# Block inverse of a gated delta net with its four series alternating, and the output transposes moved into the projection (two-layer hybrid attention, one core)

## The chip, the cores and the metric

One core of a Trainium2 chip (trn2) runs the whole program. The metric is the device time of one execution in microseconds (us), given as the median of several executions; the profile comes from one further execution of its own. TensorE is PE in the profile, with its weight loads as PEld, VectorE is DVE, ScalarE is ACT, GpSimd is POOL, and SyncE is SP, which here only issues transfers.

## What is computed

Two layers on x (256 tokens, width 2048), all in fp32. Layer 0 joins a gated delta net (8 heads, run in both directions), a differential attention (8 heads) and a memory attention, and adds their projection to x; layer 1 is sliding-window, latent and memory attention in the same frame. The part that matters here is the delta net of layer 0:

```python
m = jnp.where(strict, jnp.einsum('bhncd,bhnsd->bhncs', k_beta, k) * decay, 0.0)
t_inv = lax.linalg.triangular_solve(eye + m, jnp.broadcast_to(eye, m.shape), left_side=True, lower=True,
                                    unit_diagonal=True)
u = t_inv @ (v * beta[..., None])
w = t_inv @ (k_beta * jnp.exp(g)[..., None])
...
o = rms_norm(o, out_gain) * jax.nn.silu(gate.reshape(bsz, seq, GDN_HEADS, GDN_DV).astype(F32))
...
return x + y @ w_out
```

The kernel takes chunks of 128 tokens, so it inverts a unit triangular 128x128 matrix for each head, direction and chunk. y joins the outputs of the delta net (1024 columns), the differential attention (1024) and the memory attention (512).

## The kernel before

Every weight matrix passes through `load_split`: SP loads 512 KB into `w` (L194, 4 buffers), ACT casts it to `wh` (L201), and DVE forms the rest `wl` (L202; 3 buffers of each). Three matmuls per product, high by high, low by high and high by low, then give fp32 accuracy. `gemm` (L218 to L220), `gate_T` (L361 to L363) and `gemm_out` (L250 to L252) have this form. A scheduler orders the instructions of each engine when the program is built, so that matmuls of these products fill the delta net's waits wherever it sees them free.

The delta net works on 4 heads at a time (`grp` 0, then 1). The inverses of the 32x32 diagonal blocks are computed on DVE in one buffer, `Rm`, and leave for DRAM as `t_d` and `r_d` (L794 to L797). POOL then clears `Rm` (L800), and for each group four transfers bring the blocks back into `Tm` and four into `Rm` (L812): `Tm` holds the transposed inverse, `Rm` the inverse. Two steps build the 128x128 inverse. The first joins pairs of 32x32 blocks: PX (L849, `M8` and `T8` into `px`), a copy to `X1` on DVE (L851), PY (L855, into `py`) with a copy into `T8` on ACT (L857), and PR (L860, into `pr`) with a copy into `R8` on DVE (L862). `M8`, `T8` and `R8` are views of `MnT`, `Tm` and `Rm`. The second step does the same with 64x64 blocks: PA (L869), a copy to `X2` (L870), PB (L875) and a copy into `R8` (L876).

A series is the 8 matmuls of one direction d and one pair of blocks: 4 series in each product of the first step, 2 in each of the second. An fp32 matmul leaves two records in the trace, so a series has 16 and a product of the first step 64. The operands of the four series come from four different groups of 32 partitions. `px` and `py` of one direction share a PSUM bank, and `pr` has another, so that two of the four series always write to one bank.

After the inverse a chain of small products runs in `bank4`: L889 on PE, L898 and L899, L902 (the copy to `St`, ACT), L906, L910, L914, then L919 and L921. L178 (ACT) sums squares, L145 (POOL) takes the root, and L929 writes `o_gdn`, which L348 multiplies by the gate. `gated_T` transposes it (L388) and splits it into `y[0]` and `y[4]` (L154 ACT, L155 DVE). `gemm_out` walks over four groups of 512 columns, and in each over the blocks 8, 12, 16, 0 and 4 of y, in chunks of two k-tiles of 12 matmuls each; blocks 0 and 4 are the delta net's, the others those of the two attentions.

Of the kernel before, what the change touches and what calls it, by code (L numbers as in the profile page):

```python
# [36 lines left out]
R_GDN, R_SUB, R_EMQ, R_EMK, R_OMQ, R_OMK, R_SWQ, R_SWK, R_MLQ, R_MLK, R_DFQ, R_DFK, R_CNV = range(68, 81)  # L37
# [50 lines left out]
def kernel(ctx: ExitStack, tc: tile.TileContext, a: dict, out: bass.AP):  # L88
    nc = tc.nc
    V, A, G, T = nc.vector, nc.scalar, nc.gpsimd, nc.tensor  # L90
# [17 lines left out]
    def ps_tile():  # L108
        return psp.tile([P, 512], F32, tag="ps", name="ps")
# [87 lines left out]
    def load_split(src, kn, n):  # L197
        w = first_w.pop(0) if first_w else load_w(src, kn, n)
        wh = wpool.tile([P, KC * 512], F32R, tag="wh", name="wh")
        wl = wpool.tile([P, KC * 512], F32R, tag="wl", name="wl")  # L200
        A.copy(wh[:, :kn * n], w[:, :kn * n])  # L201
        V.tensor_tensor(wl[:, :kn * n], w[:, :kn * n], wh[:, :kn * n].bitcast(F32), op=ALU.subtract)  # L202
        return (wh[:, :kn * n].rearrange("p (k n) -> p k n", k=kn),
                wl[:, :kn * n].rearrange("p (k n) -> p k n", k=kn))
# [30 lines left out]
                T.matmul(o, lhsT=wl[:, k], rhs=H[:, kk], start=False, stop=kk == NK - 1)  # L235
        return acc

    def gemm_out(wd, y, blocks, evac):

        wv = wd.rearrange("(k p) c -> p k c", p=P)  # L240
        chunks = [(k0, k) for k0 in blocks for k in range(0, 4, KC)]
        for g in range(D // 512):
            acc = [accp.tile([P, 512], F32, tag="acc", name="acc") for _ in range(2)]
            for b, (k0, ks) in enumerate(chunks):
                wh, wl = load_split(wv[:, k0 + ks:k0 + ks + KC, g * 512:(g + 1) * 512], KC, 512)
                for t in range(2):
                    for k in range(KC):
                        h, l = (x_[:, ks + k, t * P:(t + 1) * P] for x_ in y[k0])
                        first, last = b == 0 and k == 0, b == len(chunks) - 1 and k == KC - 1
                        T.matmul(acc[t], lhsT=h, rhs=wh[:, k], start=first, stop=False)  # L250
                        T.matmul(acc[t], lhsT=h, rhs=wl[:, k], start=False, stop=False)  # L251
                        T.matmul(acc[t], lhsT=l, rhs=wh[:, k], start=False, stop=last)  # L252
            for t in range(2):
                evac(g, t, acc[t])
# [127 lines left out]
    def gated_T(o_get, gain, y):  # L382

        for t in range(2):
            pt = accp.tile([P, 512], F32, tag="acc", name="acc")
            o_ = o_get(t)
            for c in range(4):
                T.transpose(pt[:, c * P:(c + 1) * P], o_[:, c * P:(c + 1) * P], ident)  # L388
            src = pt.rearrange("p (c q) -> p c q", c=4)
            split(src, gain, *(x_[:, :, t * P:(t + 1) * P] for x_ in y))  # L390


    par = keep(R_END)
# [283 lines left out]
    o_gdn = opool2.tile([P, 2, 1024], F32, name="o_gdn")  # L677
# [124 lines left out]
    for grp in range(2):  # L802
# [27 lines left out]
        for t in range(2):  # L830
# [3 lines left out]
            for h in range(4):  # L834
# [8 lines left out]
        px, py, pr = [[p_[d].rearrange("p (m c) -> p m c", m=8) for d in range(2)]  # L843
                      for p_ in ([b_[0][:, :S] for b_ in banks], [b_[0][:, S:] for b_ in banks],
                                 [b_[1][:, :S] for b_ in banks])]
        for d in range(2):
            for r_, c_ in rcs[d]:
                for m in range(8):
                    T.matmul(px[d][blk[r_], m], lhsT=M8[d][blk[c_], m, blk[r_]], rhs=T8[d][blk[c_], m, blk[c_]],  # L849
                             start=True, stop=True)  # L850
                V.tensor_copy(X1[d][blk[r_], :, 0:32], px[d][blk[r_]])  # L851
        for d in range(2):
            for r_, c_ in rcs[d]:
                for m in range(8):
                    T.matmul(py[d][blk[r_], m], lhsT=R8[d][blk[r_], m, blk[r_]], rhs=X1[d][blk[r_], m, 0:32],  # L855
                             start=True, stop=True)
                A.copy(T8[d][blk[r_], :, blk[c_]], py[d][blk[r_]])  # L857
            for r_, c_ in rcs[d]:
                for m in range(8):
                    T.matmul(pr[d][blk[c_], m], lhsT=X1[d][blk[r_], m, 0:32], rhs=R8[d][blk[r_], m, blk[r_]],  # L860
                             start=True, stop=True)
                V.tensor_copy(R8[d][blk[c_], :, blk[r_]], pr[d][blk[c_]])  # L862
        rc2 = [(slice(64, 128), slice(0, 64)), (slice(0, 64), slice(64, 128))]
        X2 = [gp.tile([P, 8, 64], F32, tag="X", name="X2", bufs=2) for d in range(2)]
        for d in range(2):
            r_, c_ = rc2[d]
            pa = ps_tile().rearrange("p (m c) -> p m c", m=8)
            for m in range(8):
                T.matmul(pa[r_, m], lhsT=M8[d][c_, m, r_], rhs=T8[d][c_, m, c_], start=True, stop=True)  # L869
            V.tensor_copy(X2[d][r_], pa[r_])  # L870
        for d in range(2):
            r_, c_ = rc2[d]
            pb = ps_tile().rearrange("p (m c) -> p m c", m=8)
            for m in range(8):
                T.matmul(pb[c_, m], lhsT=X2[d][r_, m], rhs=R8[d][r_, m, r_], start=True, stop=True)  # L875
            A.copy(R8[d][c_, :, r_], pb[c_])  # L876

# [55 lines left out]
    def cols512(x_, g):  # L935
        return lambda t: x_[:, t, 512 * g:512 * (g + 1)]
# [16 lines left out]
    with tc.tile_pool(name="yp", bufs=2, reuse_waits="tile") as yp:  # L953
        y = {k: halves(yp, [P, 4, S], f"y{k}", bufs=1) for k in range(0, 20, 4)}
        for g in range(2):
            gated_T(cols512(o_dif, g), par[:, R_SUB:R_SUB + 1], y[8 + 4 * g])
        split(o_mem, None, *y[16])
        for i in range(2):
            gated_T(cols512(o_gdn, i), par[:, R_GDN:R_GDN + 1], y[4 * i])

        ssx = yp.tile([P, 2, 4], F32, name="ssx1", bufs=1)
        nxt = []

        def evac(g, t, ps):
            if not nxt:
                nxt.extend(xpool.tile([P, NK, S], F32R, tag=n, name=n + "1") for n in ("xH", "xL"))
            x_ = x1[:, t, 512 * g:512 * (g + 1)]
            xr = yp.tile([P, 512], F32, tag="xr", name="xr")
            with tc.issue_after(acts[-1].ins):
                A.dma_start(xr, a["xN"][t * P:(t + 1) * P, 512 * g:512 * (g + 1)])  # L970
            V.tensor_tensor(x_, ps, xr, op=ALU.add)
            sum_sq(x_, ssx[:, t, g:g + 1], [P, 512])
            if t == 1:
                split_T(lambda k, t: x1[:, t, k * P:(k + 1) * P], par[:, R_ODN:R_ODN + NK], range(4 * g, 4 * g + 4), *nxt)
        gemm_out(a["ev_w_out"][0], y, (8, 12, 16, 0, 4), evac)
        opool_stack.close()
        xH, xL = nxt
        ss1 = spool.tile([P, 2], F32, tag="ssx", name="ss1")
        V.tensor_reduce(ss1, ssx, axis=AX.X, op=ALU.add)
        inv_sqrt(rs1, ss1, 1.0 / D, EPS)  # L980
# [9 lines left out]
    y = {}  # L990
# [210 lines left out]
```

## Time and profile before

| | us |
|---|---|
| median of 3 runs | 1225.27 (1223.86 to 1230.07) |
| profiled execution | 1225.94 |
| its span in the trace | 1224.2 |
| PE busy | 1203.8 |
| DVE busy | 841.3 |
| ACT busy | 640.8 |
| POOL busy | 107.8 |

The span runs from the first to the last instruction of the trace; the execution's own time lies 1.74 us above it. The mean granted clock of TensorE is 0.992 of full speed. A row of a timeline has start, duration, engine, line, operation, output and inputs, tile and count; rows of one line that follow each other are joined, and brackets name idle time ahead of the row and what ended it.

### The profile page before, as it was taken

How to read it: one execution, taken by the hardware profiler on the slowest of the kernel's cores; microseconds unless marked ns; L12 is line 12 of the kernel's file. 1: busy time of each engine (PE TensorE's matmuls, PEld its weight loads, DVE VectorE, ACT ScalarE, POOL GpSimd, SP SyncE). 2: the span in 40 equal slices, each digit the busy share in tenths (PEclk: the TensorE clock that was granted, in tenths of full speed). 3: DMA queues.
4: the chain of work that ended last, by engine and by line, in shares of the span. 5: the costliest groups of instructions: out<-in, count | busy, mean ns of one | idle time of the engine just before them, and what ended most of it. 6: DMA issues, size and time to landing. Idle time of an engine off the chain costs nothing.

```text
span 1224.2 us, 19860 instructions
## 1 busy us (share of the span) xinstructions
PE 1203.8 (98%) x7608; PEld 1075.8 (88%) x7608; DVE 841.3 (69%) x1450; ACT 640.8 (52%) x1117; POOL 107.8 (9%) x116
## 2 busy tenths in 40 slices
PE   9899999999999999999979999999999999999998
PEld 7678878788999998899968889999889889998887
DVE  6766876576989899738645555577666677776553
ACT  6754755455555454334644445666555455554332
POOL 0110102010001010002000000332200000000000
PEclk9999999999999999989989999999999999999999
DMA  9976766546655676723516656666656565554663
GB/s 339 356 225 227 231 203 180 172 146 181 170 158 137 158 193 189 204 81 91 167 50 208 206 184 165 189 182 191 174 155 207 151 206 160 158 161 165 205 207 120
DMA packets 183184, 221.95 MB, mean 181 GB/s; under 512 B 20537, under 2 KB 119609, under 8 KB 182577
## 3 DMA queue, kind: packets, MB, share of 16 engines
q1 hardware_dynamic: 172640, 201.09, 55.0%
q10 hardware_dynamic: 9552, 16.48, 3.8%
q0 software_dynamic: 896, 3.11, 0.8%
q8 instruction: 59, 0.97, 0.3%
q14 instruction: 37, 0.30, 0.1%
HBM read 214.36 MB, written 6.29 MB: 180 GB/s over the span
## 4 chain that ended last, share of the span: by engine, by line
PE 87%; DMA 5%; DVE 4%; ACT 2%; issue 1%; POOL 0%; SPq 0%; ACTq 0%; DVEq 0%
PE acc L219 13%; PE acc L218 12%; PE acc L220 12%; PE acc L251 6%; PE acc L250 6%; PE acc L252 6%; PE acc L362 4%; PE acc L363 4%; PE acc L361 4%; PE acc L235 3%; PE acc L233 3%; PE acc L234 3%; PE ps L165 3%; DMA w<-in_ev_w_in_dram 2%; PE ps L889 2%; DVE wl L202 2%
## 5 line engine op out<-in xcount | busy, mean ns | idle before, releaser
L202 DVE TENSOR_TENSOR wl<-w,wh 128x1024 fp32r<-128x1024 f32 (+3 forms) x392 | 456.8, 1167 | 246.1 <-ACT wh L201 239.5
L201 ACT CAST wh<-w 128x1024 fp32r<-128x1024 f32 (+3 forms) x392 | 391.9, 1001 | 405.8 <-PE acc L220 138.5
L219 PE MATMUL acc<-wl,xH 128*128 128x512 f32 (+3 forms) x704 | 258.1, 368 | 3.2 <-DVE wl L202 3.2
L220 PE MATMUL acc<-wh,xL 128*128 128x512 f32 (+3 forms) x704 | 254.9, 363 | 0.0
L218 PE MATMUL acc<-wh,xH 128*128 128x512 f32 (+3 forms) x704 | 238.0, 366 | 3.3 <-ACT wh L201 3.3
L219 PEld LDWEIGHTS acc<-wl,xH 128*128 128x128 f32 x704 | 132.3, 188 | 24.0 <-DVE wl L202 5.5
L218 PEld LDWEIGHTS acc<-wh,xH 128*128 128x128 f32 x704 | 129.9, 188 | 21.9 <-ACT wh L201 5.0
L220 PEld LDWEIGHTS acc<-wh,xL 128*128 128x128 f32 x704 | 132.3, 188 | 16.8
L251 PE MATMUL acc<-wl,y 128*128 128x512 f32 x320 | 125.0, 391 | 0.0
L252 PE MATMUL acc<-wh,y 128*128 128x512 f32 x320 | 124.6, 391 | 0.0
L250 PE MATMUL acc<-wh,y 128*128 128x512 f32 x320 | 114.8, 392 | 0.0
L362 PE MATMUL acc<-xL,wh 128*128 128x256 f32 x384 | 110.5, 288 | 0.0
L361 PE MATMUL acc<-xH,wh 128*128 128x256 f32 x384 | 110.4, 288 | 0.0
L235 PE MATMUL acc<-xH,wl 128*128 128x256 f32 x384 | 109.4, 286 | 0.8 <-DVE wl L202 0.8
L363 PE MATMUL acc<-xH,wl 128*128 128x256 f32 x384 | 110.0, 287 | 0.0
L233 PE MATMUL acc<-xH,wh 128*128 128x256 f32 x384 | 109.3, 285 | 0.0
L234 PE MATMUL acc<-xL,wh 128*128 128x256 f32 x384 | 109.1, 284 | 0.0
L145 POOL TENSOR_TENSOR r<-isq,kept 128x4 f32<-128x4 f32 (+2 forms) x27 | 51.2, 1895 | 394.8 <-DVE isq L144 390.2
L362 PEld LDWEIGHTS acc<-xL,wh 128*128 128x128 f32 x384 | 74.7, 194 | 0.4
L361 PEld LDWEIGHTS acc<-xH,wh 128*128 128x128 f32 x384 | 74.7, 195 | 0.2
L235 PEld LDWEIGHTS acc<-xH,wl 128*128 128x128 f32 x384 | 73.4, 191 | 1.4 <-DVE wl L202 1.4
L363 PEld LDWEIGHTS acc<-xH,wl 128*128 128x128 f32 x384 | 74.6, 195 | 0.0
(364 smaller groups left out, 1788.5 us busy)
## 6 DMA issues: line engine op xcount, KB each, us to landing
w<-in_ev_w_in_dram SPq DMA_DIRECT2D x136, 512.0 KB, 4.0
w<-in_od_w_in_dram SPq DMA_DIRECT2D x72, 512.0 KB, 3.7
w<-in_ev_w_out_dram SPq DMA_DIRECT2D x40, 512.0 KB, 3.7
w<-in_od_w_out_dram SPq DMA_DIRECT2D x40, 512.0 KB, 3.7
w<-in_od_w_in_dram SPq DMA_DIRECT2D x32, 384.0 KB, 3.3
w<-in_od_mem_w_kv_dram SPq DMA_DIRECT2D x16, 512.0 KB, 3.6
w<-in_ev_mem_w_kv_dram SPq DMA_DIRECT2D x16, 512.0 KB, 3.7
w<-in_od_w_in_dram SPq DMA_DIRECT2D x16, 288.0 KB, 2.9
```

The lines of the kernel that those rows point to most:

```text
L201: A.copy(wh[:, :kn * n], w[:, :kn * n])
L202: V.tensor_tensor(wl[:, :kn * n], w[:, :kn * n], wh[:, :kn * n].bitcast(F32), op=ALU.subtract)
L218: T.matmul(o, lhsT=h, rhs=wh[:, k], start=first, stop=False)
L219: T.matmul(o, lhsT=h, rhs=wl[:, k], start=False, stop=False)
L220: T.matmul(o, lhsT=l, rhs=wh[:, k], start=False, stop=last)
L235: T.matmul(o, lhsT=wl[:, k], rhs=H[:, kk], start=False, stop=kk == NK - 1)
L250: T.matmul(acc[t], lhsT=h, rhs=wh[:, k], start=first, stop=False)
L251: T.matmul(acc[t], lhsT=h, rhs=wl[:, k], start=False, stop=False)
L252: T.matmul(acc[t], lhsT=l, rhs=wh[:, k], start=False, stop=last)
L361: T.matmul(acc[i], lhsT=wh[:, k, cs], rhs=H[:, kk], start=kk == 0, stop=False)
L362: T.matmul(acc[i], lhsT=wh[:, k, cs], rhs=L[:, kk], start=False, stop=False)
L363: T.matmul(acc[i], lhsT=wl[:, k, cs], rhs=H[:, kk], start=False, stop=kk == NK - 1)
```

## The change

In the block inverse the loops over the heads m and over the series are exchanged, so that the four series of PX, PY and PR, and the two of PA and PB, alternate matmul by matmul. The copies follow when all of a product's series are through. In the projection, `gated_T` of the delta net's output is no longer called ahead of `gemm_out`: `gemm_out` calls it when the first group of columns comes to block 0 and to block 4. The operations, their sizes and their operands stay as they were.

```diff
@@ -235,13 +235,17 @@
                 T.matmul(o, lhsT=wl[:, k], rhs=H[:, kk], start=False, stop=kk == NK - 1)
         return acc
 
-    def gemm_out(wd, y, blocks, evac):
-
+    def gemm_out(wd, y, blocks, evac, late=()):
+
+
+        late = dict(late)
         wv = wd.rearrange("(k p) c -> p k c", p=P)
         chunks = [(k0, k) for k0 in blocks for k in range(0, 4, KC)]
         for g in range(D // 512):
             acc = [accp.tile([P, 512], F32, tag="acc", name="acc") for _ in range(2)]
             for b, (k0, ks) in enumerate(chunks):
+                if k0 in late:
+                    late.pop(k0)()
                 wh, wl = load_split(wv[:, k0 + ks:k0 + ks + KC, g * 512:(g + 1) * 512], KC, 512)
                 for t in range(2):
                     for k in range(KC):
@@ -843,37 +847,36 @@
         px, py, pr = [[p_[d].rearrange("p (m c) -> p m c", m=8) for d in range(2)]
                       for p_ in ([b_[0][:, :S] for b_ in banks], [b_[0][:, S:] for b_ in banks],
                                  [b_[1][:, :S] for b_ in banks])]
-        for d in range(2):
-            for r_, c_ in rcs[d]:
-                for m in range(8):
-                    T.matmul(px[d][blk[r_], m], lhsT=M8[d][blk[c_], m, blk[r_]], rhs=T8[d][blk[c_], m, blk[c_]],
-                             start=True, stop=True)
-                V.tensor_copy(X1[d][blk[r_], :, 0:32], px[d][blk[r_]])
-        for d in range(2):
-            for r_, c_ in rcs[d]:
-                for m in range(8):
-                    T.matmul(py[d][blk[r_], m], lhsT=R8[d][blk[r_], m, blk[r_]], rhs=X1[d][blk[r_], m, 0:32],
-                             start=True, stop=True)
-                A.copy(T8[d][blk[r_], :, blk[c_]], py[d][blk[r_]])
-            for r_, c_ in rcs[d]:
-                for m in range(8):
-                    T.matmul(pr[d][blk[c_], m], lhsT=X1[d][blk[r_], m, 0:32], rhs=R8[d][blk[r_], m, blk[r_]],
-                             start=True, stop=True)
-                V.tensor_copy(R8[d][blk[c_], :, blk[r_]], pr[d][blk[c_]])
-        rc2 = [(slice(64, 128), slice(0, 64)), (slice(0, 64), slice(64, 128))]
+        four = [(d, blk[r_], blk[c_]) for i in range(2) for d in range(2) for r_, c_ in [rcs[d][i]]]
+        for m in range(8):
+            for d, r_, c_ in four:
+                T.matmul(px[d][r_, m], lhsT=M8[d][c_, m, r_], rhs=T8[d][c_, m, c_], start=True, stop=True)
+        for d, r_, c_ in four:
+            V.tensor_copy(X1[d][r_, :, 0:32], px[d][r_])
+        for m in range(8):
+            for d, r_, c_ in four:
+                T.matmul(py[d][r_, m], lhsT=R8[d][r_, m, r_], rhs=X1[d][r_, m, 0:32], start=True, stop=True)
+        for d, r_, c_ in four:
+            A.copy(T8[d][r_, :, c_], py[d][r_])
+        for m in range(8):
+            for d, r_, c_ in four:
+                T.matmul(pr[d][c_, m], lhsT=X1[d][r_, m, 0:32], rhs=R8[d][r_, m, r_], start=True, stop=True)
+        for d, r_, c_ in four:
+            V.tensor_copy(R8[d][c_, :, r_], pr[d][c_])
+        two = [(d, slice(64, 128), slice(0, 64)) if d == 0 else (d, slice(0, 64), slice(64, 128)) for d in range(2)]
         X2 = [gp.tile([P, 8, 64], F32, tag="X", name="X2", bufs=2) for d in range(2)]
-        for d in range(2):
-            r_, c_ = rc2[d]
-            pa = ps_tile().rearrange("p (m c) -> p m c", m=8)
-            for m in range(8):
-                T.matmul(pa[r_, m], lhsT=M8[d][c_, m, r_], rhs=T8[d][c_, m, c_], start=True, stop=True)
-            V.tensor_copy(X2[d][r_], pa[r_])
-        for d in range(2):
-            r_, c_ = rc2[d]
-            pb = ps_tile().rearrange("p (m c) -> p m c", m=8)
-            for m in range(8):
-                T.matmul(pb[c_, m], lhsT=X2[d][r_, m], rhs=R8[d][r_, m, r_], start=True, stop=True)
-            A.copy(R8[d][c_, :, r_], pb[c_])
+        pa, pb = [[ps_tile().rearrange("p (m c) -> p m c", m=8) for d in range(2)] for _ in range(2)]
+        for m in range(8):
+            for d, r_, c_ in two:
+                T.matmul(pa[d][r_, m], lhsT=M8[d][c_, m, r_], rhs=T8[d][c_, m, c_], start=True, stop=True)
+        for d, r_, c_ in two:
+            V.tensor_copy(X2[d][r_], pa[d][r_])
+        for m in range(8):
+            for d, r_, c_ in two:
+                T.matmul(pb[d][c_, m], lhsT=X2[d][r_, m], rhs=R8[d][r_, m, r_], start=True, stop=True)
+        for d, r_, c_ in two:
+            A.copy(R8[d][c_, :, r_], pb[d][c_])
@@ -955,9 +958,6 @@
         for g in range(2):
             gated_T(cols512(o_dif, g), par[:, R_SUB:R_SUB + 1], y[8 + 4 * g])
         split(o_mem, None, *y[16])
-        for i in range(2):
-            gated_T(cols512(o_gdn, i), par[:, R_GDN:R_GDN + 1], y[4 * i])
-
         ssx = yp.tile([P, 2, 4], F32, name="ssx1", bufs=1)
         nxt = []
@@ -972,7 +972,8 @@
             sum_sq(x_, ssx[:, t, g:g + 1], [P, 512])
             if t == 1:
                 split_T(lambda k, t: x1[:, t, k * P:(k + 1) * P], par[:, R_ODN:R_ODN + NK], range(4 * g, 4 * g + 4), *nxt)
-        gemm_out(a["ev_w_out"][0], y, (8, 12, 16, 0, 4), evac)
+        gemm_out(a["ev_w_out"][0], y, (8, 12, 16, 0, 4), evac,
+                 [(4 * i, lambda i=i: gated_T(cols512(o_gdn, i), par[:, R_GDN:R_GDN + 1], y[4 * i])) for i in range(2)])
         opool_stack.close()
         xH, xL = nxt
         ss1 = spool.tile([P, 2], F32, tag="ssx", name="ss1")
```

Line numbers after the change: PX is L854, PY L859, PR L864, PA L872, PB L877; `gate_T` is L365 to L367, `gemm_out` L254 to L256, the transposes L392, and the loads of Tm and Rm L816.

The scheduler also places what stands around these lines anew. TensorE, group 0, from the end of PX to PR (numbers behind names are buffers; `DMAHW` is a transfer, `x7` seven of the same form). Before, PX's third and fourth series stand apart and are followed by PR and PY:

```order
L849 MATMUL ps_4423<-Tm_3796,MnT_3258 32x32 [waits DMAHW6_49,DVE_49]
L849 MATMUL ps_4423<-Tm_3796,MnT_3258 32x32 x7
L363 MATMUL acc_5933<-xH_81,wl_5967 128x256
L361 MATMUL acc_5932<-xH_81,wh_5966 128x256
L362 MATMUL acc_5932<-xL_82,wh_5966 128x256
L363 MATMUL acc_5932<-xH_81,wl_5967 128x256
L361 MATMUL acc_5933<-xH_81,wh_5966 128x256
L849 MATMUL ps_4425<-Tm_3796,MnT_3258 32x32 [waits DMAHW7_49,DVE_49]
L849 MATMUL ps_4425<-Tm_3796,MnT_3258 32x32 x7
L860 MATMUL ps_4424<-Rm_3711,X_4421 32x32 [waits DMAHW2_49,Pool_49]
L860 MATMUL ps_4424<-Rm_3711,X_4421 32x32 x6
L855 MATMUL ps_4423<-X_4421,Rm_3711 32x32 [waits DVE_49]
```

After, PX is one piece, whose first matmuls wait for four transfers:

```order
L367 MATMUL acc_5933<-xH_81,wl_5937 128x256
L854 MATMUL ps_4423<-Tm_3796,MnT_3258 32x32 [waits DMAHW1_49]
L365 MATMUL acc_5932<-xH_81,wh_5936 128x256
L854 MATMUL ps_4425<-Tm_3796,MnT_3258 32x32 [waits DMAHW2_49]
L854 MATMUL ps_4423<-Tm_3796,MnT_3258 32x32 [waits DMAHW3_49]
L854 MATMUL ps_4423<-Tm_3796,MnT_3258 32x32 x2
L854 MATMUL ps_4425<-Tm_3796,MnT_3258 32x32 [waits DMAHW4_49]
L854 MATMUL ps_4425<-Tm_3796,MnT_3258 32x32 x2
L854 MATMUL ps_4423<-Tm_3796,MnT_3258 32x32
L854 MATMUL ps_4425<-Tm_3796,MnT_3258 32x32
```

The rest of PX goes on alternating between the two banks; 42 matmuls of `gate_T` follow, and then PY and PR as one piece.

SP, the transfers of group 0's blocks. Before:

```order
L812 DMA Tm<-t_d 32x16x32 [waits DMAHW5_49,DMAHW3_49,DMAHW1_49]
L812 DMA Tm<-t_d 32x16x32 [waits DMAHW2_49]
L796 DMA r_d<-Rm 32x1024
L194 DMA w<-in_ev_w_in_dram 128x4x256 [waits DMAHW4_49,DVE_49]
L797 DMA t_d<-Rm 32x1024
L812 DMA Tm<-t_d 32x16x32 [waits DMAHW6_49]
L812 DMA Tm<-t_d 32x16x32 [waits DMAHW7_49]
L194 DMA w<-in_ev_w_in_dram 128x4x256 [waits DMAHW0_49]
L194 DMA w<-in_ev_w_in_dram 128x4x256 [waits DMAHW1_49,DVE_49]
L812 DMA Rm<-r_d 32x16x32 [waits DMAHW3_49,DMAHW2_49,Pool_49]
L812 DMA Rm<-r_d 32x16x32
L812 DMA Rm<-r_d 32x16x32 [waits DMAHW5_49,DMAHW4_49]
```

After, the four loads of Tm stand together, ahead of the writes of `r_d` and `t_d`, and three weight loads (L194) stand ahead of the loads of Rm:

```order
L816 DMA Tm<-t_d 32x16x32 [waits DMAHW5_49,DMAHW3_49,DMAHW1_49]
L816 DMA Tm<-t_d 32x16x32 [waits DMAHW2_49]
L816 DMA Tm<-t_d 32x16x32
L816 DMA Tm<-t_d 32x16x32 [waits DMAHW4_49]
L800 DMA r_d<-Rm 32x1024
L801 DMA t_d<-Rm 32x1024 [waits DMAHW6_49]
L194 DMA w<-in_ev_w_in_dram 128x4x256 [waits DMAHW7_49,DVE_49]
L194 DMA w<-in_ev_w_in_dram 128x4x256 [waits DMAHW0_49]
L194 DMA w<-in_ev_w_in_dram 128x4x256 [waits DMAHW1_49,DVE_49]
L816 DMA Rm<-r_d 32x16x32 [waits DMAHW5_49,DMAHW2_49,Pool_49]
L816 DMA Rm<-r_d 32x16x32 [waits DMAHW3_49]
L816 DMA Rm<-r_d 32x16x32 [waits DMAHW4_49]
```

In the projection, TensorE before, from the delta net's last product (L919) to the first of `gemm_out`:

```order
L919 MATMUL ps_5570<-Tm_4709,E_3638 128x128 [waits DVE_49]
L919 MATMUL ps_5570<-Tm_4709,E_3638 128x128 x6
L388 MATMUL acc_6546<-kept_58,o_gdn_2941 128x128 [waits DVE_49]
L388 MATMUL acc_6560<-kept_58,o_gdn_2941 128x128 [waits PE_49]
L388 MATMUL acc_6560<-kept_58,o_gdn_2941 128x128 [waits DVE_49]
L388 MATMUL acc_6560<-kept_58,o_gdn_2941 128x128 x2
L388 MATMUL acc_6553<-kept_58,o_gdn_2941 128x128 [waits DVE_49]
L388 MATMUL acc_6567<-kept_58,o_gdn_2941 128x128 [waits PE_49]
L250 MATMUL acc_6575<-wh_6579,y8_6513 128x512 [waits PE_49]
L251 MATMUL acc_6575<-wl_6580,y8_6513 128x512
L252 MATMUL acc_6575<-wh_6579,y8_6513 128x512
```

TensorE after, in the middle of `gemm_out`, at its 62nd matmul:

```order
L254 MATMUL acc_6548<-wh_6641,y16_6515 128x512
L255 MATMUL acc_6548<-wl_6642,y16_6515 128x512
L256 MATMUL acc_6548<-wh_6641,y16_6515 128x512
L392 MATMUL acc_6657<-kept_58,o_gdn_2941 128x128 [waits DVE_49]
L392 MATMUL acc_6664<-kept_58,o_gdn_2941 128x128 x2
L392 MATMUL acc_6664<-kept_58,o_gdn_2941 128x128 [waits DVE_49]
L254 MATMUL acc_6547<-wh_6673,y0_6511 128x512 [waits Activation_49]
L255 MATMUL acc_6547<-wl_6674,y0_6511 128x512
L254 MATMUL acc_6548<-wh_6673,y0_6511 128x512 [waits Activation_49]
```

ACT there, after the change:

```order
L178 ACTIVATE junk_5614,ss_5606<-MnT_3639 128x128 [waits DVE_49]
L201 CAST wh_6673<-w_6671 128x1024 [waits DMAHW0_49,PE_49]
L201 CAST wh_6691<-w_6689 128x1024 [waits DMAHW1_49,PE_49]
L201 CAST wh_6723<-w_6721 128x1024 [waits DMAHW2_49,DVE_49,PE_49]
L154 ACTIVATE y0_6511<-acc_6657,kept_58 128x4x128 [waits PE_49]
L154 ACTIVATE y0_6511<-acc_6664,kept_58 128x4x128 [waits PE_49]
L154 ACTIVATE y4_6512<-acc_6707,kept_58 128x4x128 [waits PE_49]
L201 CAST wh_6741<-w_6739 128x1024 [waits DMAHW3_49,DVE_49,PE_49]
```

Before, the four splits (L154) of `y0` and `y4` followed L178 with no cast between them. Now 62 matmuls of blocks 8, 12 and 16 stand between parts of the delta net's last products and the first transpose, ten more follow it, and on ACT three casts stand between L178 and L154.

## Rows read from the trace of the kernel before

**Rows 1.** The page of the profile: busy time of the engines, and the chain.
```profile
PE 1203.8 (98%) x7608; PEld 1075.8 (88%) x7608; DVE 841.3 (69%) x1450; ACT 640.8 (52%) x1117; POOL 107.8 (9%) x116
...
PE 87%; DMA 5%; DVE 4%; ACT 2%; issue 1%; POOL 0%; SPq 0%; ACTq 0%; DVEq 0%
```

**Rows 2.** PE's waits over the whole run: total, times, longest.
```profile
PE acc L388 <- DVE o_gdn L348: 6.2, 2, 5.2
...
PE ps L860 <- DMA Rm<-r_d: 1.5, 1, 1.5
```

**Rows 3.** Windows: length, busy time of each engine, PEclk (granted clock), DMA, GB/s.
```profile
520.00:530.00 10.00, 10.00 (x128) 9.65 (x125) 2.90 (x5) 2.14 (x4) 0.00 (x0) 0.51 0.44 134
...
620.00:630.00 10.00, 5.53 (x19) 4.33 (x20) 6.07 (x15) 3.58 (x14) 2.03 (x2) 0.66 0.00 0
```

**Rows 4.** Timeline of PE, group 0's inverse.
```profile
510.76 0.28 PE L362 MATMUL acc<-xL,wh 128*128 128x256 f32 x1
510.88 0.28 PE L363 MATMUL acc<-xH,wl 128*128 128x256 f32 x1
511.09 1.09 PE L849 MATMUL ps<-Tm,MnT 32*32 32x32 f32 x32
512.12 0.38 PE L361 MATMUL acc<-xH,wh 128*128 128x256 f32 x1
512.34 0.28 PE L362 MATMUL acc<-xL,wh 128*128 128x256 f32 x1
...
525.47 0.26 PE L855 MATMUL ps<-X,Rm 32*32 32x32 f32 x1
525.49 0.27 PE L860 MATMUL ps<-Rm,X 32*32 32x32 f32 x2
...
525.67 0.88 PE L860 MATMUL ps<-Rm,X 32*32 32x32 f32 x13
...
541.87 1.16 PE L889 MATMUL ps<-vN,Rm 128*128 128x128 f32 x8
```

**Rows 5.** Timeline of PE, group 1's inverse.
```profile
573.14 0.71 PE L849 MATMUL ps<-Tm,MnT 32*32 32x32 f32 x20
...
589.71 0.19 PE L855 MATMUL ps<-X,Rm 32*32 32x32 f32 x1
589.71 0.19 PE L860 MATMUL ps<-Rm,X 32*32 32x32 f32 x1
...
594.63 1.90 PE L869 MATMUL ps<-Tm,MnT 64*64 64x64 f32 x32
...
604.62 1.16 PE L889 MATMUL ps<-vN,Rm 128*128 128x128 f32 x8
```

**Rows 6.** Groups by form on PE, group 1's inverse (572.8 to 604.6 us).
```profile
L219 PE MATMUL acc<-wl,xH 128*128 128x272 f32 x44 | 12.9, 300 | 0.0
```

**Rows 7.** Timeline of SP, group 0's blocks; then line L812, landing times.
```profile
507.93 0.85 SPq L812 DMA_DIRECT2D Tm<-t_d  x2
...
516.44 2.19 SPq L812 DMA_DIRECT2D Rm<-r_d  x4
...
DMA to landing us min/median/max: 1.9/2.5/4.1
```

**Rows 8.** Timelines of PE and ACT where the projection begins.
```profile
626.71 0.63 PE L251 MATMUL acc<-wl,y 128*128 128x512 f32 x1
627.14 0.63 PE L252 MATMUL acc<-wh,y 128*128 128x512 f32 x1
...
629.25 0.40 PE L252 MATMUL acc<-wh,y 128*128 128x512 f32 x1
629.48 0.39 PE L250 MATMUL acc<-wh,y 128*128 128x512 f32 x1
...
623.92 0.69 ACT L154 ACTIVATE y<-acc,kept 128x512 fp32r<-128x512 f32 x1 [2.41 <-PE acc L388]
...
633.47 1.05 ACT L201 CAST wh<-w 128x1024 fp32r<-128x1024 f32 x1 [0.70 <-PE acc L252]
```

## The prediction

> **What bounds the kernel now.** I read the page first: PE is busy for 1203.8 of 1224.2 us, and the chain that ended last is PE for 87% [rows 1]. An engine that is this full gains in two ways only: its work gets shorter, or its waits and slow stretches go. The list of PE's waits comes next: the longest is that of the transposes L388 for `o_gdn`, 6.2 us in two pieces, and PR's wait for its blocks is 1.5 us [rows 2]. Then the windows, for the clock: TensorE was granted 0.51 from 520 to 530 and 0.66 from 620 to 630 [rows 3], so that at 2.4 GHz otherwise it ran at 1.2 GHz after each of those waits. Last, PE's timeline of the two inverses and of the projection's start. There the reader is to look at starts, not durations: the ends of matmuls are modelled, and what a fragment costs is the distance to the next start.
>
> What a fragment of small matmuls costs shows in group 0. Matmuls of `gate_T` start 0.12 us apart, the first of PX follows after 0.21, and behind PX the second `gate_T` follows the first after 0.22 [rows 4]: some 0.1 us on either side, 0.2 for a fragment. Inside, 32 records of PX, two series one after the other, take 1.03 us, 32 ns each [rows 4]: this is the serial rate. Where series of different partitions meet they overlap: at 589.71 records of PY and PR start together [rows 5]. From 525.47 to 525.67, three series at once, ten records start in 0.20 us (one, two, and so on in turn), 20 ns each, and this at half clock [rows 4].
>
> **The change, term by term.** Nothing is removed and no instruction is added; matmuls change their order, and with them some transfers on SP and casts on ACT.
>
> *Products.* Twenty nanoseconds at half clock are 10 to 12 at full clock, so 64 alternating records take 64 x 11 = 0.7 us and an end of 0.1: 0.8 for each of PX, PY and PR, instead of 64 x 32 ns = 2.0. Four at once were never seen; the bounds are 64 x 8 + 0.1 = 0.6 (a quarter of the serial rate) and 2.0 (no overlap at all). The row with three at once is nearest. PA and PB: 32 serial records take 1.90 us [rows 5]; two at once give 0.95 and an end, 1.1, between 1.0 and 1.9.
>
> *Group 1.* The inverse takes from 572.83, just ahead of the first row, to L889 at 604.62, 31.8 us [rows 5]. In it 130 matmuls of `gemm` (three lines of 44 each, less two at the edge) [rows 6] at 0.125 make 16.3, and 24 transposes of other work, 0.13 each, 3.2. The rest, 12.3, is the inverse, in twelve fragments; from the parts it is the same, 3 x 2.0 + 2 x 1.9 + 12 x 0.2 = 12.2. After the change there are six fragments (PX in two, PY, PR, PA, PB): 3 x 0.8 + 2 x 1.1 + 6 x 0.2 = 5.8. Gain 6.5, between 5 and 8 unless a rival holds. DVE's copies of X now come after the whole product; 36 matmuls, 4.5 us, stand between PX and PY, and cover them. With that cover gone, they would show as a wait of about 1 us.
>
> *Group 0.* From the first `gate_T` at 509.57 (ten ahead of the first row) to L889 at 541.87 it is 32.3 us [rows 4]; 126 plain matmuls of 0.119 make 15.0, and 17.3 remain, with the wait of 1.5 and some 2.2 that `gate_T` lost at half clock (24 of them, 0.09 each: half clock lengthens a distance from 0.23 to 0.43 [rows 8]). After: five fragments, 3 x 0.8 + 2 x 1.1 + 5 x 0.2 = 5.6. To this come new waits, as both first products now need all of their blocks. PX comes after 12 matmuls, at 511.0; the four loads of Tm take SP from 507.93, 0.43 each, to 509.6 [rows 7], and land 2.5 us (median) behind that, up to 4.1 [rows 7]: I take 1.0 of wait, 0.5 to 2. PY then comes after 42 more, at 518.0. The loads of Rm took SP from 516.44 for 2.19 us [rows 7]; ahead of them `r_d` and `t_d` now stand behind two loads of Tm (1.0) in place of a weight load (0.4 to 0.5), so they go out about 0.4 later, end at 519.0 and land between 521.5 and 523.1. PE waits 3.5 to 5.1, less if the matmuls before are late: I take 4.3, from 2 to 5.7. A wait of 1.5 was followed by half clock for ten us [rows 2, 3]; a longer one should be too: 0.9 on PY and PR, and 2.3 on the 25 matmuls behind, from 0 to 4. Sum 5.6 + 1.0 + 4.3 + 0.9 + 2.3 = 14.1. Gain 3.2, from 0 to 8. Weight loads are moved past Rm's loads on SP and come no later than before; no `gate_T` waits for them, with 42 matmuls in hand.
>
> *Projection.* The wait for `o_gdn` (6.2) goes, and with it the half clock behind it: `gemm_out` started 0.43 us apart, not 0.23 [rows 8], six times, and some 0.5 on the transposes: 1.7. Together 7.9. Now 72 matmuls of blocks 8, 12 and 16 (0.23 each, 16.6 us) fill the chain's gaps. Two new waits stand against this, both on ACT. First, behind the matmuls for `St`, ACT has two gate evaluations (about 0.9), a cast of 1.05 and two splits of 0.69 [rows 8] ahead of the copy of `St`: 3.3, and 0.6 for the copy, while PE has some 24 matmuls of 128 columns, 2.9, of its own; with the signals about 1.4, an estimate. Second, the third cast in the order listed stands ahead of the splits of `y0` and needs the buffer that matmul 72 frees: 1.05 + 0.69 + 0.69, less the transposes (0.5) and two matmuls (0.46) that run in between, is 1.5, with signals 1.7. So 7.9 - 3.1 = 4.8; between 2.5 (half clock comes back) and 7. Weight loads and casts of `gemm_out` come sooner, when SP has been idle; they cost nothing as long as the four buffers of `w` run ahead.
>
> The sum is 6.5 + 3.2 + 4.8 = 14.5. The profiled execution of 1225.94 becomes 1211.4; it stood 0.7 above the median of the runs, so by that 1210.8: **1211 us**.
>
> **A rule against it.** Where four series alternate, the rows show up to three at once, at 20 ns a record [rows 4]; but in the row of 20 records, where series 1 and 2 overlap at full clock, starts lie (0.71 - 0.19) / 19 = 27 ns apart on average [rows 5]. The Trainium skill, "TensorE: Matmul & The Clock Gate", section "Wait - 56ns, not 53.3ns?", says that matmuls never start closer than about 25 ns apart however small; by it a product would take 64 x 25 = 1.6 us and not 0.8. The starts at 589.71, two at a time, speak against it for single records, though not for a whole product.
>
> **The rivals.**
> 1. *A floor on starts.* If records follow at 27 ns on average, as in the row of 20, a product takes 64 x 27 = 1.73, and the six lose 6 x 0.93 = 5.6: 1216.4. For it: that row; no stretch of the trace has more than ten records at a faster rate. Against: these ten, at half clock.
> 2. *One bank, one writer.* Two of the four series write to one bank; overlapping series of before always had different ones. If the two of a bank take turns, only two run at once: 64 x 16 ns + 0.1 = 1.1, 0.3 more for each of six products: 1213. The Trainium skill, "TensorEngine Tiling (Array Packing)", section "Gotcha 1: PSUM Pressure", says that row tiles cannot use one bank at the same time; no row shows it either way.
> 3. *Group 0 keeps its loss.* The loads of Rm land at 523 and half clock lasts, so that its gain of 3.2 is gone: 1214 to 1215.
> 4. *New waits in the projection.* With waits of 6 us in place of 3.1, and the half clock again, the gain of 4.8 goes to 0: 1216.
> 5. *Switching costs, the other side.* If each switch of partitions cost what entering a fragment does, 0.1, alternating would pay it at every matmul. With 32 matmuls of 0.063 in each product, (0.063 + 0.1) x 32 = 5.2 in place of 0.8, six times 26.5; for PA and PB, (0.116 + 0.1) x 16 = 3.5 in place of 1.1, four times 9.4. That is 35.9 lost against 14.5 gained, 1246.7. It decides from 0.04 a switch: 256 switches and 10 us of lost overlap then eat more than 20.6. Against it: in the ten records at 525.47 each start switches, with no such gap.
> 6. *Nothing changes.* The scheduler has filled the gaps anyway, and the overlap doesn't come: group 1 gains six fragments (1.2), the projection 3: 1221.
>
> **How the numbers follow.** The forecast gets 0.50, the floor 0.20, the bank 0.08, group 0 0.08, the projection 0.08, nothing 0.03, switching 0.03. What a measurement can tell from no change here is 0.5%, 6.1 us: below 1219.1 is faster. Only the sixth rival lies within that bound, and rival 1 with 3 or 4 together (1219 to 1221), for which I take 0.07 out of the floor's and theirs: same 0.10. Slower is the fifth alone, 0.03; faster 0.87. The range goes down to where all three terms reach their favourable ends, not quite (6 + 8 + 7 = 21, 1204), and up to the floor together with a part of group 0's loss, 1219.5.
>
> **What would show it.** Right: PX, PY and PR each within 1 us from first start to next line, PA and PB near 1.1; group 1 from 12.3 to 6 us; a wait of PE for Rm of about 4 us near 518, half clock behind it; no wait of 5 us before the transposes, `gemm_out` at 0.23 throughout, and two waits of 1 to 2 us, one for ACT before the products with `St`, one after matmul 72. Wrong: products of 1.7 (floor), of 1.1 with starts in pairs (bank), or above 2 (switching); a granted clock of 0.5 in the projection; or PE waiting for `wh` of `gemm_out`.

## The result, and the profile after

The changed kernel took 1208.04 us in the median of 4 runs (1205.23 to 1208.82), the kernel before 1224.57 (1221.41 to 1230.07): ratio 0.985, 95% interval 0.9817 to 0.9884. That is 16.5 us less, where 14.5 were forecast; the predicted time was 1211. The profiled execution took 1208.67 us, with a span of 1206.9 and a mean granted clock of 0.996 (0.992 before).

The list of PE's waits of the changed kernel (total, times, longest):

```profile
PE ps L859 <- DMA Rm<-r_d: 2.3, 1, 2.3
PE acc L254 <- ACT y L154: 1.3, 1, 1.3
...
PE ps L892 <- ACT MnT L905: 1.0, 1, 1.0
```

The 6.2 us of the transposes [rows 2] are gone; the two small waits that the prediction named are there, and the wait for `Rm` is 2.3 where it was 1.5 [rows 2]. The windows of the changed kernel say what became of the clock (length, busy time of PE, PEld, DVE, ACT, POOL, then PEclk, DMA, GB/s):

```profile
40.00:50.00 10.00, 9.96 (x31) 8.03 (x32) 7.12 (x15) 9.04 (x12) 0.72 (x1) 0.69 1.03 376
...
520.00:530.00 10.00, 8.15 (x191) 7.84 (x192) 4.83 (x7) 2.65 (x6) 0.00 (x0) 0.83 0.52 147
...
620.00:630.00 10.00, 8.69 (x43) 6.53 (x42) 5.57 (x9) 3.38 (x5) 0.00 (x0) 1.00 0.54 172
```

0.51 and 0.66 before [rows 3] have become 0.83 and 1.00. The first row is no effect of the change: this execution was granted 1.2 GHz for 6.8 us near 40 us, far ahead of the inverse and the projection, and reached the inverse 2.0 us late. The same happened, for 3.4 or 6.8 us, in ten of the fourteen profiled executions of this document, and not in those of before, e2, e4 and e5; PE's order is the same in all of them up to PX of group 0.

PE's timeline of group 0:

```profile
511.54 0.28 PE L365 MATMUL acc<-xH,wh 128*128 128x256 f32 x1
...
513.54 0.76 PE L854 MATMUL ps<-Tm,MnT 32*32 32x32 f32 x62
514.23 0.39 PE L366 MATMUL acc<-xL,wh 128*128 128x256 f32 x1
...
521.85 1.08 PE L859 MATMUL ps<-X,Rm 32*32 32x32 f32 x62 [2.32 <-DMA Rm<-r_d]
...
522.77 0.78 PE L864 MATMUL ps<-Rm,X 32*32 32x32 f32 x62
523.48 0.39 PE L366 MATMUL acc<-xL,wh 128*128 128x256 f32 x1
...
527.24 1.21 PE L872 MATMUL ps<-Tm,MnT 64*64 64x64 f32 x32
528.38 0.39 PE L366 MATMUL acc<-xL,wh 128*128 128x256 f32 x1
...
536.86 1.39 PE L892 MATMUL ps<-vN,Rm 128*128 128x128 f32 x11
```

And of group 1:

```profile
566.79 0.59 PE L854 MATMUL ps<-Tm,MnT 32*32 32x32 f32 x44
567.31 0.39 PE L219 MATMUL acc<-wl,xH 128*128 128x272 f32 x1
...
572.01 1.03 PE L859 MATMUL ps<-X,Rm 32*32 32x32 f32 x64
573.72 0.39 PE L219 MATMUL acc<-wl,xH 128*128 128x272 f32 x1 [0.67 <-DVE wl L202]
...
576.93 0.78 PE L864 MATMUL ps<-Rm,X 32*32 32x32 f32 x64
577.64 0.39 PE L219 MATMUL acc<-wl,xH 128*128 128x272 f32 x1
...
581.70 1.31 PE L872 MATMUL ps<-Tm,MnT 64*64 64x64 f32 x32
582.94 0.39 PE L219 MATMUL acc<-wl,xH 128*128 128x272 f32 x1
...
590.95 1.95 PE L892 MATMUL ps<-vN,Rm 128*128 128x128 f32 x16
```

From first start to the next line's, PX (62 records, group 0) and PR (64, group 1) take 0.7 us, PA 1.14 in group 0 and 1.24 in group 1; serially they took 2.0 and 1.8 [rows 4, 5]. PY's row is 1.03 long in group 1, where a wait follows it. Inside PX (44 records in 0.59, each 0.19 long) starts lie (0.59 - 0.19) / 43 = 9 ns apart.

Where the time went, by the same sums as in the prediction. Group 0: 511.54 to 536.86 is 25.3; 131 plain matmuls of 0.119 take 15.6; 9.7 are left of 17.3, gain 7.6. Group 1: 565.59 to 590.95 is 25.4; 138 plain matmuls of 0.1255 (17.3) and 11 transposes of 0.13 (1.4) leave 6.6 of 12.3, gain 5.7. When the starts of matched matmuls of the two executions are compared, the changed kernel is 2.0 late ahead of group 0 and 17.1 early behind the projection's start, so 19.1 in all. What remains, 19.1 - 7.6 - 5.7 = 5.8, is the projection's, and its waits say nearly the same: 6.2 and 1.7 of half clock are gone, 1.0 and 1.3 have come, 5.6 in all.

### The profile page after: what moved, and what is told of

Read it like the earlier page. It is cut to its first block, busy times and chain, and to the rows that moved or that the text cites. A ratio compares the mean times of both kernels' runs of the same rounds, so it can differ in the third digit from the quotient of the medians.

```text
span 1206.9 us, 19842 instructions
## 1 busy us (share of the span) xinstructions
PE 1190.3 (99%) x7608; PEld 1063.2 (88%) x7608; DVE 839.8 (70%) x1450; ACT 640.0 (53%) x1117; POOL 109.8 (9%) x116
## 4 chain that ended last, share of the span: by engine, by line
PE 89%; DVE 4%; DMA 3%; ACT 2%; issue 1%; POOL 1%; SPq 0%; DVEq 0%; ACTq 0%; POOLq 0%
PE acc L219 14%; PE acc L220 13%; PE acc L218 13%; PE acc L254 6%; PE acc L256 6%; PE acc L255 6%; PE acc L366 4%; PE acc L367 4%; PE acc L365 4%; PE acc L235 3%; PE acc L233 3%; PE acc L234 3%; PE ps L165 3%; PE ps L892 1%; DVE wl L202 1%
## 5 line engine op out<-in xcount | busy, mean ns | idle before, releaser
L220 PEld LDWEIGHTS acc<-wh,xL 128*128 128x128 f32 x704 | 133.1, 189 | 17.1
L256 PE MATMUL acc<-wh,y 128*128 128x512 f32 x320 | 124.4, 390 | 0.0
L254 PE MATMUL acc<-wh,y 128*128 128x512 f32 x320 | 115.3, 392 | 1.3 <-ACT y L154 1.3
L365 PE MATMUL acc<-xH,wh 128*128 128x256 f32 x384 | 110.1, 287 | 0.0
L367 PE MATMUL acc<-xH,wl 128*128 128x256 f32 x384 | 109.6, 286 | 0.0
L365 PEld LDWEIGHTS acc<-xH,wh 128*128 128x128 f32 x384 | 74.3, 194 | 0.2
L367 PEld LDWEIGHTS acc<-xH,wl 128*128 128x128 f32 x384 | 74.1, 193 | 0.0
```

What stands on the lines that cost most here:

```text
L220: T.matmul(o, lhsT=l, rhs=wh[:, k], start=False, stop=last)
L365: T.matmul(acc[i], lhsT=wh[:, k, cs], rhs=H[:, kk], start=kk == 0, stop=False)
L367: T.matmul(acc[i], lhsT=wl[:, k, cs], rhs=H[:, kk], start=False, stop=kk == NK - 1)
```

## The experiments

Two theories stood against each other in the first four runs: that the three terms add up, each for its own reason, or that one of them (order, overlap, the wait for `Rm`) carries the others. All ratios are to the kernel before; the edits are shown against the changed kernel.

**e1, the inverse alone.**

```diff
+        for i in range(2):
+            gated_T(cols512(o_gdn, i), par[:, R_GDN:R_GDN + 1], y[4 * i])
-        gemm_out(a["ev_w_out"][0], y, (8, 12, 16, 0, 4), evac, [(4 * i, lambda i=i: ...
+        gemm_out(a["ev_w_out"][0], y, (8, 12, 16, 0, 4), evac)
```

> The alternating inverse alone, with the transposes of the delta net's output ahead of the projection as before. Theory (the parts add): the two inverses keep what the aligned traces show for them, 7.8 and 6.7 us, and the projection keeps its wait of 5 to 6 us for o_gdn and the half clock behind it: 14.5 below before, about 1210, some 4.6 above the changed kernel (shift of matched matmuls past the projection -14.5, not -19). Rival (the shorter inverse also opens the projection): the wait for o_gdn is below 2 us and the time that of the changed kernel, 1208.

Measured: 1213.42 us, ratio 0.9903 (0.9869 to 0.9937). The old wait is back, to the tenth:

```profile
PE acc L392 <- DVE o_gdn L352: 6.2, 2, 5.2
```

So the inverse alone gives 12 us, 2.5 less than expected, and the projection's wait doesn't open with it.

**e2, the late transposes alone** (the inverse of before; the cut shows PX).

```diff
-        for m in range(8):
-            for d, r_, c_ in four:
...
+        for d in range(2):
+            for r_, c_ in rcs[d]:
+                for m in range(8):
```

> The late transposes alone, with the inverse of before. Theory: the projection's 4.6 us come without the inverse, about 1220, with one wait of about 1.0 for the copy of St, one of about 1.3 for the split of y0, and full clock in gemm_out. Rival: the gain needs the shorter inverse, because the chain otherwise ends too late for the 72 matmuls to cover it; then a wait for o_gdn of 3 us or more stays and the time is 1223 to 1225.

Measured: 1225.86 us over 10 runs, ratio 1.000 (0.9976 to 1.0024): nothing. The rival was right. With e1's 12 us this makes 12 of the 16.5; the others come only with both parts. PE's timeline of this kernel behind the delta net's last product (L921), from the fastest of the ten runs (1218.04, granted clock 0.999):

```profile
624.13 3.51 PE L921 MATMUL ps<-Tm,E 128*128 128x128 f32 x30
631.33 0.33 PE L390 MATMUL acc<-kept,o_gdn 128*128 128x128 f32 x1 [3.68 <-DVE o_gdn L350]
632.43 0.79 PE L252 MATMUL acc<-wh,y 128*128 128x512 f32 x1 [0.78 <-ACT y L154]
```

No matmul of the projection stands between L921 and the transpose. In this order all 72 of blocks 8, 12 and 16 were spent earlier, 23, 15, 18 and 16 of them between the chain's small products, where they hold the chain back. In the changed kernel only 34 stand there, and 28 follow the last product. This gave a theory for the next two runs: the projection gains by the matmuls that are left behind the last product to cover the 4 to 5 us to `o_gdn`.

**e8 and e9, the alternating inverse in one group only**, with late transposes.

```diff
+        if grp == 0:
...
+        else:
+            for d in range(2):
+                for r_, c_ in rcs[d]:
```

(e9 has `grp == 1`.)

> Late transposes, and the alternating inverse in group 0 only; group 1 keeps the series of before. In TensorE's order only 4 of the 72 matmuls of blocks 8, 12 and 16 are left behind the chain's last product (0 in the late transposes alone, 28 in the changed kernel). Theory (the projection gains by the matmuls that are left there to cover the 4 to 5 us to o_gdn): a wait for o_gdn of about 2.5 to 3.5 us stays, the projection gains 1 us or nothing, group 0 some 7: 1216 to 1219. Rival (group 0's shorter inverse lets the chain end sooner, and the projection's 5 us come as well): no wait for o_gdn above 1 us, 1211 to 1213.

> Late transposes, and the alternating inverse in group 1 only; group 0 keeps the series of before. Behind the chain's last product 18 of the 72 matmuls are left in TensorE's order. Theory (matmuls left there cover the way to o_gdn, 18 x 0.23 = 4.1 us of 4 to 5): the wait for o_gdn falls to 1 us or less, group 1 gains 6 to 6.5, the projection 3 to 5, group 0 nothing but what its clock does: 1213 to 1216. Rival (the projection gains only if both groups end sooner): a wait of 3 us or more for o_gdn, 1218 to 1220.

Measured: e8 1217.64 us over 10 runs, ratio 0.994 (0.9922 to 0.9957); e9 1211.18 over 7, ratio 0.9901 (0.9871 to 0.993), below the 1213 to 1216 expected. Four of e9's runs, at a granted clock of 0.997 to 0.999, took 1209.1 to 1211.2; three at 0.990 to 0.994 took 1214.6 to 1218.8. PE's timeline of e8, with 4 matmuls left:

```profile
625.46 0.39 PE L256 MATMUL acc<-wh,y 128*128 128x512 f32 x1
625.69 0.82 PE L392 MATMUL acc<-kept,o_gdn 128*128 128x128 f32 x6
629.62 0.48 PE L392 MATMUL acc<-kept,o_gdn 128*128 128x128 f32 x1 [3.10 <-DVE o_gdn L352]
```

and of e9, with 18 (the last of them, and the transposes):

```profile
626.02 0.39 PE L256 MATMUL acc<-wh,y 128*128 128x512 f32 x1
626.25 1.11 PE L392 MATMUL acc<-kept,o_gdn 128*128 128x128 f32 x6
```

With 0, 4, 18 and 28 matmuls left, the wait for `o_gdn` is 3.7, 3.1, 0 and 0. That is the theory's order, and e8 shows that a shorter inverse in group 0 doesn't help the projection. Three waits for the splits of `y`, 0.8, 0.6 and 0.7, stay in e9. Why the scheduler keeps more of them back when group 1's inverse alternates wasn't tried.

**e3, pieces kept whole, no alternation.**

```diff
-        for m in range(8):
-            for d, r_, c_ in four:
+        for d, r_, c_ in four:
+            for m in range(8):
```

(in all five products)

> As the changed kernel, but within each product one series after the other (m innermost), so that products stay in one piece and copies stay behind the whole product, with no alternation. Theory (overlap of row groups pays): PX, PY and PR take 64 x 32 ns = 2.0 us each where the changed kernel has 0.7 to 0.9, PA and PB 1.9 where it has 1.2, so 6 x 1.2 + 4 x 0.7 = 10 us slower than the changed kernel: 1218. Rival (fewer fragments and the new order of the transfers pay): within 2 us of the changed kernel, 1208 to 1210.

Measured: 1218.49 us over 10 runs, ratio 0.994 (0.9921 to 0.996), 10 above the changed kernel. The products are as expected. PE's timeline of e3, PX of group 0, PY and PA of group 1:

```profile
509.84 1.91 PE L854 MATMUL ps<-Tm,MnT 32*32 32x32 f32 x64
...
577.35 1.85 PE L859 MATMUL ps<-X,Rm 32*32 32x32 f32 x64
...
587.50 1.90 PE L872 MATMUL ps<-Tm,MnT 64*64 64x64 f32 x32
```

But the ten us don't lie where I put them. Matched matmuls of the two profiled executions put some 10 us into group 0 and 0.8 into all behind it. Half clock in group 0 lasted 17 us in place of 3.4; its windows:

```profile
520.00:530.00 10.00, 10.00 (x136) 9.25 (x134) 2.94 (x6) 1.45 (x4) 0.00 (x0) 0.57 0.35 120
530.00:540.00 10.00, 10.00 (x66) 9.31 (x66) 1.76 (x3) 2.49 (x4) 0.00 (x0) 0.57 0.12 30
```

In group 1 the products lose their 4 us, and the projection gives most of it back: the waits for `St` and for `y0` don't occur in e3's order. Nor is the half clock one execution's: all ten runs of e3 were granted 0.987 to 0.992, the four of the changed kernel 0.996 to 0.998. Overlap is shown by the durations; that it is worth 10 us by itself is not.

**e5, e6 and e11, two series at a time**: of one bank (e5; e11 is the same kernel again, with four runs) and of two banks (e6), in PX, PY and PR.

```diff
-        for m in range(8):
-            for d, r_, c_ in four:
+        pairs = [(m, s_) for h_ in (four[0::2], four[1::2]) for m in range(8) for s_ in h_]
+        for m, (d, r_, c_) in pairs:
```

(e6: `four[0:2], four[2:4]`)

> As the changed kernel, but in PX, PY and PR only two series alternate at a time, the two that write to the same PSUM bank (both of one direction), first direction 0, then 1. Theory (partitions alone decide, a shared bank costs nothing): two at once, 64 records at 16 to 17 ns, about 1.1 us from first start to the next line. Rival (one bank takes one writer at a time): they take turns, 32 ns, 2.0 to 2.1 us.

> As the changed kernel, but in PX, PY and PR only two series alternate at a time, the two of different directions, so of different PSUM banks. Both theories: 16 to 17 ns a record, about 1.1 us for each product. Against the pairs of one bank: equal if partitions alone decide, half of it if the bank does. Time some 6 x 0.3 = 2 us above the changed kernel, 1210.

> The pairs of one bank once more, with more rounds. Theory (its order leaves no wait for Rm, St or y0): 1203 to 1206, as in the first look. Rival (that look had luck with the clock, which was granted in full throughout): 1207 to 1209, as the changed kernel.

PX of group 0 with pairs of one bank (e5):

```profile
510.49 1.10 PE L855 MATMUL ps<-Tm,MnT 32*32 32x32 f32 x62
511.52 0.38 PE L366 MATMUL acc<-xL,wh 128*128 128x256 f32 x1
```

and with pairs of two banks (e6):

```profile
511.98 1.11 PE L855 MATMUL ps<-Tm,MnT 32*32 32x32 f32 x64
513.02 0.38 PE L365 MATMUL acc<-xH,wh 128*128 128x256 f32 x1
```

Some 16 ns a record in both, from first start to the next line's: the bank costs nothing here, partitions decide. Times: e5 1205.01 (2 runs), e6 1207.75 (2 runs), e11 1209.72 (4 runs; ratio 0.9874, 0.9834 to 0.9914). The two runs of e5 had luck with the clock (1.000 and 0.996, e11's four 0.994 to 0.997), as e11's rival said: two at a time are no faster than four.

**e4, e10 and e12, the wait for `Rm`.** e4 splits the clearing, e10 does it with the pairs of e5, e12 moves the loads of `Rm` to POOL's queue.

```diff
-    G.memset(Rm, 0.0)
+    G.memset(Rm[:, 0], 0.0)
+    V.memset(Rm[:, 1], 0.0)
...
-                nc.sync.dma_start(dv_[b * 32:(b + 1) * 32, :, b * 32:(b + 1) * 32], ...
+                (G if dst is Rm else nc.sync).dma_start(dv_[b * 32:(b + 1) * 32, :, b * 32:(b + 1) * 32], ...
```

> As the changed kernel, but POOL clears only one half of Rm and VectorE the other. Theory (the clearing of Rm is on the way to PY of group 0): the loads of Rm go out 0.9 us earlier, PE's wait of 2.3 falls to 1.4 or below, 1 to 2 us faster with some of the half clock: 1206 to 1207. Rival (the wait is that of the loads behind the weight loads on the queue, or VectorE's own queue holds X's copies back behind the clearing): same or up to 3 us slower, 1208 to 1211.

> Pairs of one bank as in the run before, and Rm cleared by POOL and VectorE, each one half. Behind the chain's last product 23 matmuls of the projection are left, and matmuls of the gate stand between its products. Theory (what is left of waits in the changed kernel, 2.3 for Rm, 1.0 for St, 1.3 for y0 and 0.7 behind PY, is set by the order that the pieces get, not by the products): none of these waits above 0.5 us, and 2 to 5 us less than the changed kernel: 1203 to 1206. Rival (pairs cost 0.3 us in each of six products and VectorE's share of the clearing holds X's copies back): same as the changed kernel, 1207 to 1209.

> As the changed kernel, but the eight loads of Rm are issued by POOL (GpSimd) right behind its clearing of Rm, not by SP behind three weight loads; the inverse and the projection keep TensorE's order of the changed kernel. Theory (Rm's loads land late, 5.2 us behind their issue against 2.5 in the median before, because they stand behind 1.5 MB of weights on SP's queue): they land within 3 us, TensorE's wait of 2.3 falls below 0.5 and most of its half clock with it, 2 to 4 us faster: 1204 to 1206. Rival (the 16 engines are full whatever the queue, or POOL's issue is slow): the wait stays at 2 us or grows, 1208 to 1211.

Measured: e4 1205.35 us, ratio 0.9843 (0.981 to 0.9875); e10 1210.04, 0.9874 (0.9832 to 0.9916); e12 1207.08, 0.9847 (0.9813 to 0.9881). None can be told from the changed kernel's 0.985. In e4 the loads go out 0.6 us earlier, not 0.9, and a wait of 1.9 stays in the same place (e10: 2.0, where none above 0.5 was expected), though the profile puts it down to a split on DVE. For e12, DMA issues from 508 to 524 us (KB each, median us to landing), first the changed kernel:

```profile
w<-in_ev_w_in_dram SPq DMA_DIRECT2D x5, 512.0 KB, 5.0
...
Rm<-r_d SPq DMA_DIRECT2D x4, 64.0 KB, 5.2
```

then e12:

```profile
w<-in_ev_w_in_dram SPq DMA_DIRECT2D x5, 512.0 KB, 6.5
...
Rm<-r_d POOLq DMA_DIRECT2D x4, 64.0 KB, 7.1
```

The loads go out 2.6 us earlier, counted from the first `gate_T`, because SP now writes `t_d` ahead of the loads of `Tm` and the clearing starts earlier. They take 1.9 longer, and PY starts 10.2 us behind the first `gate_T`, where the changed kernel has 10.3; PE waits 1.9. So the rival holds: leaving SP's queue doesn't bring them sooner. Of its two causes, full engines or POOL's issue, the trace speaks for the first: POOL's four issues were over by 514.5, and the first load landed at 519.3. The 16 engines were full meanwhile (window as above, DMA share the last number but one):

```profile
516.00:518.00 2.00, 2.00 (x17) 1.80 (x16) 0.70 (x1) 1.03 (x1) 0.00 (x0) 1.00 1.09 259
```

Before, when the loads landed 2.6 us (median) behind their issue, they were not:

```profile
516.00:518.00 2.00, 1.86 (x36) 1.57 (x32) 0.56 (x3) 0.00 (x0) 0.41 (x1) 1.00 0.62 169
```

That the loads share the engines with the weights is thus the likeliest reading; a run without those weight loads was not made, so it isn't shown.

**e7, the calls moved ahead**: that for `y0` by one block, that for `y4` by three.

```diff
-                 [(4 * i, lambda i=i: gated_T(
+                 [(16 - 4 * i, lambda i=i: gated_T(
```

> As the changed kernel, but the projection calls the transposes of y4 when it comes to block 12 and of y0 when it comes to block 16. Theory (the wait of 1.3 for the split of y0 is the third cast ahead of it on ScalarE, and that order stays): the wait of 1.3 stays, time within 1 us of the changed kernel, 1207 to 1209. Rival (the call's place sets the wait): the wait is below 0.5, 1 to 2 us faster, 1206 to 1207.

Measured: 1205.98 us, ratio 0.9834 (0.9782 to 0.9885), equal to the changed kernel. The wait for the split is 1.1, and one of 0.8 for DVE's half of the split comes to it. All 16 transposes stand behind the 72 matmuls now, not the first four behind 62. An earlier call doesn't shorten the wait.

## Why the prediction was right, point by point

The direction, the size and the two main mechanisms held. The single terms were off in both directions, and that their errors met so near the measured time is in part luck, with the clock above all (below).

- *Products.* Forecast 0.8 and 1.1; PX and PR 0.7, PA 1.14 and 1.24. The floor on starts is refuted by 64 records at 9 ns in place of 27 (PR of group 1), the bank by PX of e5, switching costs by both. The Trainium skill, "TensorE: Matmul & The Clock Gate", section "Wait - 56ns, not 53.3ns?", has 25 ns as the least distance of starts: it doesn't hold for small matmuls on different partitions here. PY took 1.03 in group 1: that 36 matmuls cover DVE's copies of X was too much. DVE had other work first, and its last copy began at 571.88, just ahead of PY at 572.01, and took 0.42. PY's row is 0.25 us longer than PR's, and the wait of 0.67 behind PY is for DVE as well.
- *Group 1.* 5.7 against 6.5: that wait and the longer PY are about the difference.
- *Group 0.* 7.6 against 3.2: this is the step that was mis-sized, by three of its terms. The wait for `Tm`, forecast 1.0, was 0. The wait for `Rm`, forecast 4.3, was 2.3. And half clock, forecast as "ten us" after the model of before, lasted 3.4 and cost 1.4 in place of 3.2. The rest took 6.0, forecast 5.6. For `Rm` I let `t_d` land as late after its issue as before. SP and POOL of the changed kernel; the clearing starts 0.23 us behind the landing of `t_d`, as it does in e1, e3, e5, e6, e7, e8 and e11 (0.2 each), though the row names DVE:

```profile
512.09 0.42 SPq L801 DMA_DIRECT2D t_d<-Rm  x1
512.61 1.57 SPq L194 DMA_DIRECT2D w<-in_ev_w_in_dram  x3
516.23 3.73 SPq L816 DMA_DIRECT2D Rm<-r_d  x4
```

```profile
514.40 1.80 POOL L804 MEMSET Rm<- 128x2048 f32 x1 [80.86 <-DVE o_dif L352]
```

  With the weight load now behind it, the clearing began 2.3 us after its issue (512.09 to 514.40); before, with one ahead of it, 4.8 us (509.84 to 514.60). The loads of `Rm` then went out at 516.23, 4.7 us after the first `gate_T` and not 7.3 as I had reckoned. From there to PY it was 5.6 us, forecast 5.5 (516.8 to 522.3), so that nearly all of the 2.6 came through: 2.0 off the wait, the rest off the time ahead of it, where the wait for `Tm` didn't come.
- *Projection.* 5.8 against 4.8. Both new waits came where they were said to be, 1.0 (forecast 1.4) and 1.29 (1.7). PE behind matmul 72, and ACT's third cast ahead of the splits:

```profile
625.50 0.50 PE L254 MATMUL acc<-wh,y 128*128 128x512 f32 x1 [1.29 <-ACT y L154]
```

```profile
623.82 1.04 ACT L201 CAST wh<-w 128x1024 fp32r<-128x1024 f32 x1 [2.17 <-PE acc L256]
624.77 1.26 ACT L154 ACTIVATE y<-acc,kept 128x512 fp32r<-128x512 f32 x2
```

  What the prediction missed is the condition. It treated the projection as a term of its own. e2 shows that by itself it is worth nothing.

How much of the 16.5 us is the clock? In the profiled executions half clock lasted 10.2 and 6.8 us in the two places before, 3.4 and 0 after. The granted clock of the single runs says more. Over the 53 runs of the kernel before that went with the experiments, the time falls by some 1.1 us for each 0.001 of it; the two at 0.996 and 0.997 took 1220.7 and 1218.5, and the changed kernel at the same values 1208.7, 1208.8 and 1207.4. So 11 to 12 us come at an equal clock, and about 5 with a higher one. By the same rate, an estimate, some 7 of e3's 10 us go with its lower clock. The prediction had 0.7 for the clock (2.2 and 1.7 gained, 3.2 lost) and 13.8 for the rest: the rest came out lower, the clock higher. In e2, whose group 0 has the instructions of before in the same order, neither the wait for `Rm` nor half clock occurred there, and group 0 was 6.0 us shorter than in the profile of before; that execution was the fastest of e2's ten. So group 0's 7.6 is partly a matter of what an execution meets.

## What to carry to other kernels

Small matmuls that use different partitions of the array should alternate one by one: four series then cost what one and a half did serially (0.7 us), whether or not two of them share a bank. A transposition moved behind other work pays only if that work is still there when the long latency comes; count in the order listing how many ready matmuls stand behind the chain's last product, not how many there are in all. And look at which large loads are under way with a small one, before moving it to another queue: in e12 the other queue didn't bring it sooner.

## What was not expected

- 64 records of four series start 9 ns apart at full clock, less than a third of the 32 ns of one series; two at a time 16 ns, with one bank or two. In the trace's single starts the round stays at 32 ns: 31 to 32 from record to record in series, 7 and 25 in turn with two (PR of group 0 in e5 and e6), 6, 7, 7 and 12 with four (PX of group 1). Alternating puts one record of every series into the time that a single series takes for one.
- A wait of 2.3 us was followed by 3.4 us at half clock, one of 1.5 before by 10.2, one of 1.8 in e3, with serial products behind it, by 17; after similar waits in e6 (1.4), e7 and e8 (1.9) full clock stayed. Of the twelve profiles with a wait of 1.2 to 2.6 us in group 0, nine show half clock behind it; the two without (e2, e5) don't. The length of the wait doesn't tell what the clock will do.
- Four loads of 64 KB issued 2.6 us earlier from another queue took 7.1 us in place of 5.2, and the last landed no sooner.
